# A two-layer hybrid decoder trunk: x, weights and parameters laid out by the host before the launch

## The chip, the cores and the metric

The kernel runs on one core of a Trainium2 chip. The metric is the time of one execution on the device, in microseconds (us). Engines are named as in the profile: PE multiplies matrices (PEld loads its stationary operand beside it), DVE and ACT work on vectors, POOL is a third vector engine, SP issues most of the loads.

## The reference

The input x is 512 tokens by 1024 features in float32. Each of two layers does the following.

- RMSNorm, then one input projection whose columns feed four groups of heads: forgetting attention (fox), gated linear attention (gla), multi-head latent attention with a rotary key (mla), and a Mamba-2 SSD mixer with a causal convolution (ssm).
- The four results, 256 wide each, go side by side through one output projection and are added to x.
- RMSNorm, a SwiGLU FFN with 2816 hidden units, and a second addition to x.

A final RMSNorm ends it. What the change touches is how the first of these steps begins:

```python
def rmsnorm(x, g):
    y = x * lax.rsqrt(jnp.mean(x * x, axis=-1, keepdims=True) + EPS)
    return y * g
x1 = rmsnorm(x, norm1[l]) @ w_in[l]      # 512 x 1024 times 1024 x 3000
```

## The kernel before, in words

**Tiling.** The residual x is held turned, as eight tiles `xT[k]` of 128 features by 512 tokens. Every projection is made of matmuls with a 128x128 block of the weight as the stationary operand and 512 tokens moving, summed over k in one bank of PSUM. To keep float32 accuracy, each operand is split into a high part and the remainder (`h`, `l`), and each block takes three matmuls: high by high, low by high, high by low (`prod`, L369 to L371).

**Weights.** `Weights` (L250) is a queue of units of up to 128x1024 numbers, in order of use. A unit is loaded by SP into one of two raw tiles `wr`. It is then split: ACT copies the high part `wh` (L276), DVE subtracts to get `wl` (L277), into one of three pairs of tiles. `get` keeps two units split ahead. A unit that is one 128-column block of `w_in` is read from the array as it lies, in pieces of 128 numbers (512 bytes). Small columns (gates, low rank, rotary key) are gathered by six loads into a unit that POOL has set to zero (`add_small`, L312). The two up-projections of mla are split in pieces, which also puts their columns in order (`add_mla`, L281 and L282).

**The start.** The order of the first steps on PE, DVE and ACT is written out by hand in the string `FIRST`. `T` turns one 128-feature chunk of x with four PE transposes against the identity, since x lies token by token (L917). `N` makes the two parts of a chunk, times the gain of the norm (L417, L418). `A` and `B` split the first and second half of one of the two first units. `P` does the three matmuls of one chunk for one of the two first projections. `X` and `Y` copy the turned chunk to `xT`; `Q` squares a chunk on ACT and adds it up on POOL (L941, L943); `R` makes the token-wise factor r of the norm from the sum. The factor is applied behind the projections, so PE can begin before it is known; it is spread over the partitions by one PE matmul (`spread`, L444). Before all this PE does seven warm-up matmuls on ones (`WARM`, L142).

**Parameters.** The gains and other vectors come as rows, are turned on PE and copied (`prn` at L143, `load_vectors` from L178: ten loads issued by ACT). The biases and the SSD's A and D come as four broadcasts to 128 partitions, issued by POOL (L199). Positions are loaded by POOL too (L227).

**Order.** Behind the written-out block, a planner puts instructions into each engine's order, by its own estimate of when each can run; projections run on PE while generators (`Runner`) feed the mixers' steps in between. SP's loads run in the order in which they are issued.

Of the kernel before, what the change touches and what calls it, by code (L numbers as in the profile page):

```python
# [20 lines left out]
P = 128  # L22
T = 512
# [16 lines left out]
WARM = 7  # L40
# [5 lines left out]
FIRST = """T0 T1 N0 A0 T2 N1 P00 B0 T3 N2 P01 Y0 P02 N3 T4 P03 A1 Y1 T5 P10 B1 N4 P11 P12 X2 P13 N5 Q0 T6 P04 P14 Q1 Q2  # L46
X3 N6 P05 P15 T7 Q3 Q4 W2 X4 N7 P06 P16 Q5 X5 Q6 P07 P17 Q7 X6 X7 W3 R0"""
# [11 lines left out]
def _consts():  # L59

    c = np.zeros((P, 2), np.float32)
    d = np.arange(P) % 32
    c[:, 0] = _rope_inv()[d % 16]
    c[:, 1] = np.where(d < 16, -1.0, 1.0)
    return c
# [14 lines left out]
def trunk(tc, I, out, depth=2):  # L80
# [7 lines left out]
    with ExitStack() as es:  # L88
# [26 lines left out]
        xb = []  # L115

        def load_x(n):
            for k in range(len(xb), n):
                t = tmp("a", f"x_{k}")
                nc.sync.dma_start(t.rearrange("p (b c) -> p b c", b=NB),  # L120
                                  I["x"][0].rearrange("(b p) c -> p b c", p=P)[:, :, blk(k)])
                xb.append(t)

        load_x(2)

        prn = tmp("f", "prn", P, parts=16)
        nc.scalar.dma_start(prn, I["norm1"].rearrange("l (k p) -> (l k) p", p=P))
        pcn = cp.tile([P, 16], F32, name="pcn")
        pcv = cp.tile([P, 98], F32, name="pcv")
        col = lambda i: pcn[:, i:i + 1] if i < 16 else pcv[:, i - 16:i - 15]  # L130
# [12 lines left out]
        PE.transpose(pps[:, 0:16], prn, ident[0:16, 0:16])  # L143
        V.tensor_copy(pcn, pps[:, 0:16])
# [33 lines left out]
        def load_vectors():  # L178
            prow = tmp("f", "prow", P)
            for r0, src in ((0, I["norm2"].rearrange("l (k p) -> (l k) p", p=P)),  # L180
                            (16, I["ssm_conv_w"].rearrange("l t (k p) -> (l t k) p", p=P)),
                            (64, I["ssm_conv_b"].rearrange("l (k p) -> (l k) p", p=P)),
                            (76, I["gla_gate_b"]),
                            (78, I["mla_q_norm"].rearrange("l (k p) -> (l k) p", p=P)),
                            (82, I["mla_kv_norm"]),
                            (84, I["ssm_norm"].rearrange("l (k p) -> (l k) p", p=P)),
                            (88, I["final_norm"].rearrange("(k p) -> k p", p=P))):
                n = src.shape[0]
                nc.scalar.dma_start(prow[r0:r0 + n, :], src)
            for half in range(2):  # L190
                nc.scalar.dma_start(prow[96:98, blk(half, 64)], I["gla_out_norm"])
            ps = ps_mix("ppv")
            PE.transpose(ps[:, 0:98], prow[0:98], ident[0:98, 0:98])
            V.tensor_copy(pcv, ps[:, 0:98])


        bc = cp.tile([P, 2, 16], F32, name="bc")
        for i, nm in enumerate(("fox_f_bias", "ssm_dt_bias", "ssm_A_log", "ssm_D")):
            nc.gpsimd.dma_start(bc[:, :, 4 * i:4 * i + 4], I[nm].unsqueeze(0).broadcast_to((P, 2, 4)))  # L199
        rc = cp.tile([P, 2], F32, name="rc")  # L200


        dcol = cp.tile([P, 2, 2], F32, name="dcol")
# [5 lines left out]
        def gate_constants():  # L209
            V.memset(gsgn[:, 0:4], -1.0)  # L210
            V.memset(gsgn[:, 4:8], 1.0)
            V.tensor_tensor(gbias, bc[:, :, 0:8], gsgn.unsqueeze(1).broadcast_to((P, 2, 8)), op=ALU.mult)
            V.memset(gfac, -1.0)
            S.activation(gfac[:, :, 4:8], bc[:, :, 8:12], AF.Exp)
            V.tensor_scalar(gfac[:, :, 4:8], gfac[:, :, 4:8], -1.0, None, op0=ALU.mult)
            for c in range(2):
                for hh in range(2):
                    V.tensor_copy(dcol[blk(hh, 64), :, c:c + 1],
                                  bc[blk(hh, 64), :, 12 + 2 * c + hh:13 + 2 * c + hh])
# [30 lines left out]
        class Weights:  # L250


            def __init__(self):
                self.queue, self.loaded, self.ready, self.n = [], [], [], 0

            def add(self, load, nk, ncol, pack=None):
                self.queue.append((load, nk, ncol, pack))

            def load(self):
                load, nk, ncol, pack = self.queue.pop(0)  # L260
                i, n = self.n, nk * ncol
                self.n += 1
                raw = wp.tile([P, 1024], F32, tag="wr", bufs=RAWS, name=f"wr{i}")
                load(raw[:, :n].rearrange("p (k c) -> p k c", k=nk), raw)
                self.loaded.append((raw, i, nk, ncol, pack))

            def split(self, pieces=1):

                if not self.loaded:
                    self.load()  # L270
                raw, i, nk, ncol, pack = self.loaded.pop(0)
                n = nk * ncol
                h, lo = (wp.tile([P, 1024], F32R, tag=f"w{c}", bufs=PARTS, name=f"w{c}{i}") for c in "hl")
                if pack is None:
                    for c in (blk(j, n // pieces) for j in range(pieces)):
                        S.copy(h[:, c], raw[:, c])  # L276
                        V.tensor_tensor(lo[:, c], raw[:, c], h.bitcast(F32)[:, c], op=ALU.subtract)  # L277
                        yield h, lo
                else:
                    for dst, src in pack:  # L280
                        S.copy(dst(h), src(raw))  # L281
                        V.tensor_tensor(dst(lo), src(raw), dst(h.bitcast(F32)), op=ALU.subtract)  # L282
                    nk, ncol = pack_shape[nk, ncol]
                    n = nk * ncol
                self.ready.append(tuple(t[:, :n].rearrange("p (k c) -> p k c", k=nk) for t in (h, lo)))

            def prefetch(self, n):
                while (self.queue or self.loaded) and len(self.ready) < n:
                    for _ in self.split():
                        pass  # L290
# [6 lines left out]

        pack_shape = {(2, 384): (2, 512), (1, 512): (1, 512)}

        def add_block(*srcs):  # L300

            nk = sum(s.shape[0] for s in srcs) // P

            def load(v, raw):
                k = 0
                for s in srcs:
                    n = s.shape[0] // P
                    nc.sync.dma_start(v[:, k:k + n, :], s.rearrange("(k p) c -> p k c", p=P))
                    k += n
            W.add(load, nk, srcs[0].shape[1])  # L310

        def add_small(l):  # L312
            def load(v, raw):
                G.memset(raw, 0.0)
                w = I["w_in"][l].rearrange("(k p) c -> p k c", p=P)
                for dst, src, n in ((0, FF, 4), (4, SDT, 4), (32, GG, 16), (64, MKR, 32), (96, MKR + 16, 16),
                                    (112, MKR, 16)):
                    nc.sync.dma_start(v[:, :, dst:dst + n], w[:, :, src:src + n])
            W.add(load, KC, P)

        def add_mla(l):

            v8 = lambda t, n: t[:, :8 * n].rearrange("p (k c) -> p k c", k=8)
            cut = lambda a, n, w: (lambda t: v8(t, w)[:, :, a:a + n])
            W.add(lambda v, raw: nc.sync.dma_start(v, I["mla_w_uq"][l].rearrange("(k p) c -> p k c", p=P)), 2, 384,
                  [(cut(d0, n, 128), cut(s0, n, 96)) for d0, s0, n in ((0, 0, 96), (96, 80, 16), (112, 64, 16))])

            dst = lambda i: (lambda t: t[:, blk(i, 256)].rearrange("p (h c) -> p h c", h=4))
            src = lambda i: (lambda t: t[:, :512].rearrange("p (h c) -> p h c", h=4)[:, :, blk(i, 64)])
            W.add(lambda v, raw: nc.sync.dma_start(raw[:, :512], I["mla_w_ukv"][l]), 1, 512,  # L330
                  [(dst(i), src(i)) for i in range(2)])

        def layer_weights(l):
            win, wout = I["w_in"][l], I["w_out"][l]
            cols = lambda c0: add_block(win[:, c0:c0 + P])
            for c0 in FRONT_COLS[:2]:
                cols(c0)
            add_small(l)
            for c0 in FRONT_COLS[2:] + (FK, FQ):
                cols(c0)  # L340
            tok = lambda c0: (add_block(win[0:512, c0:c0 + 256]), add_block(win[512:1024, c0:c0 + 256]))
            tok(FV)
            for c0 in (FK + P, FQ + P, MCKV, MCQ, MCQ + P, GQ, GK):
                cols(c0)
            tok(GV)
            add_mla(l)
            for i in range(4):
# [856 lines left out]
```

## Time and profile before

| | us |
|---|---|
| median of 3 runs | 1283.63 (1283.08 to 1284.28) |
| the profiled execution, its own time | 1284.61 |
| its span, from the first to the last instruction | 1282.9 |
| PE busy | 1253.4 (98%) |
| DVE busy | 697.2 (54%) |
| ACT busy | 534.5 (42%) |
| POOL busy | 195.5 (15%) |

The busy times of engines overlap. The mean granted clock of PE is 0.989 of full speed. 109.41 MB are moved in 207396 packets, 203896 of them smaller than 2 KB, at a mean of 85 GB/s.

### The profile page before, as it was taken

The page shows a single profiled execution, that of the slowest core. Times are in us where ns is not written, and L with a number is a line of the kernel's source. Part 1 is how long each engine was busy: PE and PEld are TensorE (multiplying, and loading weights), DVE is VectorE, ACT ScalarE, POOL GpSimd, SP SyncE. Part 2 cuts the span into 40 slices and gives each one's busy share as a digit, 9 for nine tenths or more (in the row PEclk, how much of TensorE's full clock was granted, in tenths as well). Part 3 has the DMA queues.
Part 4 walks back from the last instruction along what each step waited for, and adds up shares of the span by engine and source line. Part 5 has one row for each costly group of instructions (what it writes and reads, how often), then busy time and mean ns, then how long its engine had stood idle before and what let it go on. Part 6 is the DMA issues. An engine that isn't in the chain of part 4 may idle for free.

```text
span 1282.9 us, 16334 instructions
## 1 busy us (share of the span) xinstructions
PE 1253.4 (98%) x6414; PEld 1017.2 (79%) x6414; DVE 697.2 (54%) x1144; ACT 534.5 (42%) x890; POOL 195.5 (15%) x178
## 2 busy tenths in 40 slices
PE   7999999999999999999999999999999999999997
PEld 5788787678888888888888877777688888888886
DVE  5786698584343344343457677966644334433444
ACT  4456774743221222223444577565432222212232
POOL 4112221031110110011201022000311001101111
PEclk7999999999999999999999999999899999999999
DMA  7333212122333333333343221112233333333331
GB/s 135 102 99 83 58 34 79 38 75 86 99 99 99 97 90 92 100 99 91 90 98 95 69 81 53 60 42 66 66 99 99 99 99 99 89 100 99 95 90 70
DMA packets 207396, 109.41 MB, mean 85 GB/s; under 512 B 16872, under 2 KB 203896, under 8 KB 207320
## 3 DMA queue, kind: packets, MB, share of 16 engines
q1 hardware_dynamic: 206304, 107.95, 29.6%
q0 software_dynamic: 816, 0.36, 0.4%
q8 instruction: 50, 0.82, 0.3%
q14 instruction: 26, 0.21, 0.1%
q10 hardware_dynamic: 200, 0.06, 0.0%
HBM read 106.19 MB, written 2.10 MB: 84 GB/s over the span
## 4 chain that ended last, share of the span: by engine, by line
PE 90%; DVE 5%; ACT 2%; DMA 1%; issue 1%; POOL 1%; SPq 0%; DVEq 0%; ACTq 0%; POOLq 0%
PE u L369 6%; PE u L370 6%; PE u L371 6%; PE g L371 6%; PE g L369 6%; PE g L370 6%; PE d L369 5%; PE d L370 5%; PE d L371 5%; PE ft L370 3%; PE ft L369 3%; PE ft L371 3%; PE sm L745 1%; PE oa L370 1%; PE oa L369 1%; PE oa L371 1%
## 5 line engine op out<-in xcount | busy, mean ns | idle before, releaser
L276 ACT CAST wh<-wr 128x1024 fp32r<-128x1024 f32 (+2 forms) x202 | 206.8, 1025 | 567.4 <-issue 256.2
L277 DVE TENSOR_TENSOR wl<-wr,wh 128x1024 fp32r<-128x1024 f32 (+2 forms) x202 | 245.9, 1218 | 78.9 <-ACT wh L276 78.6
L369 PE MATMUL d<-uh,wh 128*128 128x512 f32 x296 | 115.1, 389 | 0.0
L370 PE MATMUL d<-uh,wl 128*128 128x512 f32 x296 | 115.1, 389 | 0.0
L371 PE MATMUL d<-ul,wh 128*128 128x512 f32 x296 | 115.1, 389 | 0.0
L1163 DVE TENSOR_TENSOR ft<-u,fs 128x512 f32<-128x512 f32 x44 | 30.4, 692 | 133.1 <-PE u L371 127.4
L1177 DVE TENSOR_TENSOR xT<-xT,d 128x512 f32<-128x512 f32 x40 | 27.5, 687 | 104.6 <-PE d L371 104.6
L1160 POOL TENSOR_TENSOR fs<-fs,n_0r 128x512 f32<-128x512 f32 x22 | 38.3, 1743 | 279.4 <-ACT fs L1159 279.4
L1160 POOL TENSOR_TENSOR fs<-fs,n_1r 128x512 f32<-128x512 f32 x22 | 38.1, 1734 | 280.5 <-ACT fs L1159 280.5
L371 PE MATMUL g<-n_1l,wh 128*128 128x512 f32 x176 | 69.0, 392 | 2.3 <-DVE n_1l L418 2.3
L371 PE MATMUL g<-n_0l,wh 128*128 128x512 f32 x176 | 68.7, 390 | 2.3 <-DVE n_0l L418 2.3
L369 PE MATMUL g<-n_0h,wh 128*128 128x512 f32 x176 | 69.0, 392 | 0.8 <-ACT n_0h L417 0.8
L369 PE MATMUL g<-n_1h,wh 128*128 128x512 f32 x176 | 69.0, 392 | 0.8 <-ACT n_1h L417 0.8
L370 PE MATMUL u<-n_1h,wl 128*128 128x512 f32 x176 | 69.4, 395 | 0.0
L369 PE MATMUL u<-n_1h,wh 128*128 128x512 f32 x176 | 69.4, 394 | 0.0
L371 PE MATMUL u<-n_1l,wh 128*128 128x512 f32 x176 | 69.3, 394 | 0.0
L370 PE MATMUL u<-n_0h,wl 128*128 128x512 f32 x176 | 69.2, 393 | 0.0
L369 PE MATMUL u<-n_0h,wh 128*128 128x512 f32 x176 | 69.1, 393 | 0.0
L371 PE MATMUL u<-n_0l,wh 128*128 128x512 f32 x176 | 69.0, 392 | 0.0
L370 PE MATMUL g<-n_1h,wl 128*128 128x512 f32 x176 | 68.5, 389 | 0.0
L370 PE MATMUL g<-n_0h,wl 128*128 128x512 f32 x176 | 68.5, 389 | 0.0
L371 PEld LDWEIGHTS d<-ul,wh 128*128 128x128 f32 x296 | 55.6, 188 | 11.6
(640 smaller groups left out, 2862.2 us busy)
## 6 DMA issues: line engine op xcount, KB each, us to landing
wr<-in_w_in_dram SPq DMA_DIRECT2D x46, 512.0 KB
wr<-in_w_gate_dram SPq DMA_DIRECT2D x44, 512.0 KB
wr<-in_w_up_dram SPq DMA_DIRECT2D x44, 512.0 KB
wr<-in_w_down_dram SPq DMA_DIRECT2D x32, 448.0 KB
wr<-in_w_down_dram SPq DMA_DIRECT2D x16, 512.0 KB
wr<-in_w_out_dram SPq DMA_DIRECT2D x16, 256.0 KB
wr<-in_w_out_dram SPq DMA_DIRECT2D x8, 512.0 KB
x<-in_x_dram SPq DMA_DIRECT2D x8, 256.0 KB
```

What stands on the lines that cost most here:

```text
L276: S.copy(h[:, c], raw[:, c])
L277: V.tensor_tensor(lo[:, c], raw[:, c], h.bitcast(F32)[:, c], op=ALU.subtract)
L369: PE.matmul(ps, lhsT=wh[:, k, c0:c0 + P], rhs=ah, start=k == 0, stop=False)
L370: PE.matmul(ps, lhsT=wl[:, k, c0:c0 + P], rhs=ah, start=False, stop=False)
L371: last = PE.matmul(ps, lhsT=wh[:, k, c0:c0 + P], rhs=al, start=False, stop=k == n - 1)
L745: PE.matmul(ps[:, :n], lhsT=q[:d, blk(qb)], rhs=k[:d, :n], start=i == 0, stop=i == len(terms[h]) - 1)
L1160: G.tensor_tensor(s, s, r, op=ALU.mult)
L1163: V.tensor_tensor(t, pu, s, op=ALU.mult)
L1177: V.tensor_tensor(xT[m], xT[m], ps, op=ALU.add)
```

## The change

The host lays out the inputs before the launch. x comes as eight blocks of 128 features by 512 tokens. Weights come as one array of units in order of use, 128 rows of 1024 numbers (4 KB) each, with the small columns and the mla columns already in place. All parameters come as one array of 152 columns. In the kernel, the turning of x, of the parameters, the broadcasts and the gathering loads are gone. SP issues x chunks and halves of the first two units by turns. Warm-up matmuls are 14 and not 7. The written-out order changes; the squares are summed on DVE, behind the split of the third unit, and the sum over features is a PE matmul (`columns`) as in the second layer. Positions are loaded by ACT.

```diff
-WARM = 7
+WARM = 14
-FIRST = """T0 T1 N0 A0 T2 N1 P00 B0 T3 N2 P01 Y0 P02 N3 T4 P03 A1 Y1 T5 P10 B1 N4 P11 P12 X2 P13 N5 Q0 T6 P04 P14 Q1 Q2
-X3 N6 P05 P15 T7 Q3 Q4 W2 X4 N7 P06 P16 Q5 X5 Q6 P07 P17 Q7 X6 X7 W3 R0"""
+FIRST = """N0 A0 P00 N1 A1 P10 P01 P11 N2 P02 P12 B0 N3 P03 P13 B1 N4 P04 P14 N5 P05 P15 N6 P06 P16 N7 P07 P17 W2 Q0 Q1 Q2 Q3
+Q4 Q5 Q6 Q7"""
+def _unit(w):
+    k = w.shape[0] // P
+    return w.reshape(k, P, -1).transpose(1, 0, 2).reshape(P, -1)
+def _weights(I, depth=2):
+    units, shapes = [], []
+    def add(*ws):
+        u = np.concatenate([_unit(w) for w in ws], 1)
+        shapes.append((u.shape[1] // ws[0].shape[1], ws[0].shape[1]))
+        units.append(np.pad(u, ((0, 0), (0, 1024 - u.shape[1]))))
...
+    return np.stack(units), shapes
+        def load_x(k):
+            nc.sync.dma_start(xT[k], I["x"][k])
+        pcv = cp.tile([P, 176], F32, name="pcv")
+        nc.scalar.dma_start(pcv[:, :152], I["columns"])
...
-            nc.gpsimd.dma_start(posi, I["positions"].broadcast_to((P, T)))
-            nc.gpsimd.dma_start(rc, I["rope_const"])
+            nc.scalar.dma_start(posi, I["positions"].broadcast_to((P, T)))
...
+            def load(self, parts=1):
+                i, (nk, ncol) = self.n, shapes[self.n]
+                self.n += 1
                 raw = wp.tile([P, 1024], F32, tag="wr", bufs=RAWS, name=f"wr{i}")
+                self.loaded.append((raw, i, nk, ncol))
+                for c in (blk(j, nk * ncol // parts) for j in range(parts)):
+                    nc.sync.dma_start(raw[:, c], I["weights"][i][:, c])
+                    yield
...
-            def square(self, k):
+            def square(self, k, adds=None):
...
-                    (V if k == KC - 1 else G).tensor_tensor(self.acc, self.acc, sq, op=ALU.add)
+                    (adds or (V if k == KC - 1 else G)).tensor_tensor(self.acc, self.acc, sq, op=ALU.add)
+                    return square
...
-        W.load()
-        load_x(4)
-        W.load()
-        load_x(KC)
+        loads = [W.load(2), W.load(2)]
+        for k in range(KC):
+            load_x(k)
+            if k < 4:
+                next(loads[k % 2])
+        for w in loads:
+            list(w)
...
             elif op[0] == "Q":
-                sq = tmp("f", f"xq{k}") if k else acc
-                S.activation(sq, xb[k], AF.Square)
-                if k:
-                    return G.tensor_tensor(acc, acc, sq, op=ALU.add)
+                squares = norm.square(k, V)
+                return squares
 
         with tc.manual_schedule(engines=ORDERED):
-            squares = None
             for op in FIRST.split():
-                squares = first(op) or squares
-            r = norm.spread()
+                squares = first(op)
+        norm.columns()
+        r = norm.spread()
         selectors()
-        load_vectors()
         gate_constants()
```

## Rows read from the trace of the kernel before

**Rows 1.** The page, part 1: busy us, share of the span, instructions.
```profile
PE 1253.4 (98%) x6414; PEld 1017.2 (79%) x6414; DVE 697.2 (54%) x1144; ACT 534.5 (42%) x890; POOL 195.5 (15%) x178
```

**Rows 2.** Table by stretches: stretch, its length, busy by engine, PEclk, DMA share, GB/s.
```profile
5.80:11.50 5.70, 0.00 (x0) 0.00 (x0) 1.00 (x3) 1.04 (x3) 0.82 (x2) 0.71 1.08 158
...
16.40:21.80 5.40, 5.38 (x17) 4.50 (x18) 2.29 (x6) 2.98 (x6) 0.00 (x0) 0.50 0.84 173
...
21.80:38.00 16.20, 16.12 (x76) 12.81 (x75) 14.01 (x19) 9.45 (x15) 12.55 (x10) 1.00 0.59 122
38.00:39.60 1.60, 0.00 (x0) 0.00 (x0) 1.18 (x4) 0.23 (x2) 0.00 (x0) 1.00 0.70 96
39.60:85.00 45.40, 45.37 (x204) 36.90 (x205) 36.95 (x74) 22.14 (x28) 3.69 (x7) 1.00 0.40 106
...
280.00:290.00 10.00, 6.80 (x24) 4.71 (x23) 8.87 (x9) 3.15 (x5) 4.41 (x3) 0.90 0.36 105
644.80:655.70 10.90, 10.90 (x51) 9.03 (x49) 3.17 (x4) 2.66 (x4) 0.18 (x1) 1.00 0.50 108
```

**Rows 3.** The chain of waits in order of time: start us, us, what.
```profile
3.08 13.29 DMA x<-in_x_dram
...
85.24 0.87 PE xt L542 x8
...
655.83 0.79 PE n_1ms L435 x8
...
660.87 0.86 PE n_1sp L444 x2
...
708.18 0.87 PE xt L542 x8
```

**Rows 4.** Instructions in order of time, SP's issues and PE: start us, us, engine, line.
```profile
0.82 0.98 SPq L120 DMA_DIRECT2D x<-in_x_dram  x2
...
1.13 3.36 PE L142 MATMUL pps<-ones 128*128 128x128 f32 x14 [1.13 <-DVE ones L134]
...
4.64 1.14 PE L917 MATMUL xt<-ident,x 128*128 128x128 f32 x8
...
5.53 3.36 SPq L308 DMA_DIRECT2D wr<-in_w_in_dram  x1
...
8.94 8.25 SPq L120 DMA_DIRECT2D x<-in_x_dram  x4
...
16.42 1.11 PE L917 MATMUL xt<-ident,x 128*128 128x128 f32 x4 [2.48 <-DMA x<-in_x_dram]
```

**Rows 5.** DMA queues in 0:20, 2:4, 8:12 and 1276:1279: packets, MB, share of 16 engines.
```profile
DMA packets 7122, 3.13 MB, mean 157 GB/s; under 512 B 1065, under 2 KB 7122, under 8 KB 7122
...
q1 hardware_dynamic: 1010, 0.50, 84.5%
...
q0 software_dynamic: 77, 0.01, 58.1%
q1 hardware_dynamic: 1096, 0.55, 53.4%
...
q1 hardware_dynamic: 228, 0.43, 39.0%
```

**Rows 6.** Groups of instructions by line and shape, 0 to 42 us: busy us, mean ns.
```profile
L418 DVE SCALAR_TENSOR_TENSOR n_0l<-xt,pcn,n_0h 128x512 fp32r<-128x512 f32 x8 | 6.0, 749 | 5.9 <-ACT n_0h L417 5.8
L417 ACT ACTIVATE n_0h<-xt,pcn 128x512 fp32r<-128x512 f32 x8 | 5.5, 688 | 10.3 <-PE xt L917 10.3
...
L941 ACT ACTIVATE xq<-x 128x512 f32<-128x512 f32 x7 | 4.0, 622 | 0.0
...
L277 DVE TENSOR_TENSOR wl<-wr,wh 128x512 fp32r<-128x512 f32 x4 | 2.7, 686 | 4.5 <-ACT wh L276 4.5
L276 ACT CAST wh<-wr 128x512 fp32r<-128x512 f32 x4 | 2.5, 614 | 4.7 <-DMA wr<-in_w_in_dram 4.7
```

**Rows 7.** One line, L282, both layers: duration ns min/median/max, first and last start, forms.
```profile
L282 DVE TENSOR_TENSOR wl<-wr,wh x10: 267/415/1372, 173.5 to 813.2; 128x128 fp32r<-128x128 f32 x4, 128x256 fp32r<-128x256 f32 x4, 128x768 fp32r<-128x768 f32 x2
```

More of the change, by code (lines that the diff above doesn't have):

```diff
@@ L56, in _rope_inv @@
     return np.float32(10000.0) ** (-(np.arange(16, dtype=np.float32) / np.float32(16.0)))
[L59 to L65, printed above, removed]
+def _unit(w):
[7 more added lines that the diff above has]
+        units.append(np.pad(u, ((0, 0), (0, 1024 - u.shape[1]))))
+    for l in range(depth):
+        win, wout = I["w_in"][l], I["w_out"][l]
+        cols = lambda c0: add(win[:, c0:c0 + P])
+        for c0 in FRONT_COLS[:2]:
+            cols(c0)
+        small = np.zeros((D, P), np.float32)
+        for dst, src, n in ((0, FF, 4), (4, SDT, 4), (32, GG, 16), (64, MKR, 32), (96, MKR + 16, 16), (112, MKR, 16)):
+            small[:, dst:dst + n] = win[:, src:src + n]
+        add(small)
+        for c0 in FRONT_COLS[2:] + (FK, FQ):
+            cols(c0)
+        tok = lambda c0: (add(win[0:512, c0:c0 + 256]), add(win[512:1024, c0:c0 + 256]))
+        tok(FV)
+        for c0 in (FK + P, FQ + P, MCKV, MCQ, MCQ + P, GQ, GK):
+            cols(c0)
+        tok(GV)
+        uq = I["mla_w_uq"][l].reshape(256, 4, 96)
+        add(np.concatenate([uq, uq[:, :, 80:96], uq[:, :, 64:80]], 2).reshape(256, 512))
+        add(I["mla_w_ukv"][l].reshape(P, 4, 2, 64).transpose(0, 2, 1, 3).reshape(P, 512))
+        for i in range(4):
+            add(wout[768:1024, 256 * i:256 * i + 256], wout[0:256, 256 * i:256 * i + 256])
+        for r0 in (256, 512):
+            for i in range(2):
+                add(wout[r0:r0 + 256, 512 * i:512 * i + 512])
+        for j0, j1 in HID_PARTS:
+            for j in range(j0, j1):
+                add(I["w_gate"][l][:, j * P:j * P + P])
+                add(I["w_up"][l][:, j * P:j * P + P])
+            for m in range(KC):
+                add(I["w_down"][l, j0 * P:j1 * P, m * P:m * P + P])
+    return np.stack(units), shapes
@@ L77, in _pieces, with trunk @@
     return out
-def trunk(tc, I, out, depth=2):
+def trunk(tc, I, out, shapes, depth=2):
     nc = tc.nc
@@ L253, in __init__ @@
             def __init__(self):
[L254 to L261, printed above, removed]
+                self.loaded, self.ready, self.n = [], [], 0
+            def load(self, parts=1):
+                i, (nk, ncol) = self.n, shapes[self.n]
@@ L269, in split @@
                 if not self.loaded:
-                    self.load()
-                raw, i, nk, ncol, pack = self.loaded.pop(0)
+                    list(self.load())
+                raw, i, nk, ncol = self.loaded.pop(0)
                 n = nk * ncol
                 h, lo = (wp.tile([P, 1024], F32R, tag=f"w{c}", bufs=PARTS, name=f"w{c}{i}") for c in "hl")
[L274 to L284, printed above, removed]
+                for c in (blk(j, n // pieces) for j in range(pieces)):
+                    S.copy(h[:, c], raw[:, c])
+                    V.tensor_tensor(lo[:, c], raw[:, c], h.bitcast(F32)[:, c], op=ALU.subtract)
+                    yield h, lo
@@ L285, in split @@
                 self.ready.append(tuple(t[:, :n].rearrange("p (k c) -> p k c", k=nk) for t in (h, lo)))
             def prefetch(self, n):
-                while (self.queue or self.loaded) and len(self.ready) < n:
+                while (self.n < len(shapes) or self.loaded) and len(self.ready) < n:
                     for _ in self.split():
@@ L296, in trunk @@
         W = Weights()
[L298 to L331, printed above, removed]
@@ L359, in trunk @@
-        for l in range(depth):
-            layer_weights(l)
         def prod(ps, w, act, c0=0, ks=None, t=slice(0, T), nk=None):
@@ L1190 @@
     from concourse.bass_utils import run_bass_kernel_spmd
+    inputs = {n: np.asarray(inputs[n]) for n in _INS}
     nc = bacc.Bacc("TRN2", target_bir_lowering=False, num_devices=1, dynamic_dma_scratch_size=4096)
-    arrays = {f"in_{n}_dram": np.ascontiguousarray(inputs[n]) for n in _INS}
-    arrays["in_rope_const_dram"] = _consts()
-    I = {}
-    for n in _INS + ["rope_const"]:
-        a = arrays[f"in_{n}_dram"]
+    units, shapes = _weights(inputs)
+    laid = {"x": np.ascontiguousarray(inputs["x"][0].T).reshape(KC, P, T), "positions": inputs["positions"],
+            "columns": _columns(inputs), "gla_gate_w2": inputs["gla_gate_w2"], "weights": units}
+    arrays, I = {}, {}
+    for n, a in laid.items():
+        arrays[f"in_{n}_dram"] = a = np.ascontiguousarray(a)
         I[n] = nc.dram_tensor(f"in_{n}_dram", a.shape, mybir.dt.from_np(a.dtype), kind="ExternalInput").ap()
@@ L1200 @@
     with tile.TileContext(nc) as tc:
-        trunk(tc, I, out)
+        trunk(tc, I, out, shapes)
     r = run_bass_kernel_spmd(nc, [arrays], core_ids=[0])
```

104 lines of the change are left out of this document (18 added, 86 removed).

## The prediction

> **What bounds the kernel now.** I read the busy table first: PE is busy 98% of the 1282.9 us span [rows 1], so only time in which PE stands or runs at its lower clock can be won. Then the table by stretches, to find that time [rows 2]. Nearly all that this change can reach lies ahead of 40 us. PE does nothing from 5.8 to 11.5 us, runs at the lower of its two levels (granted 0.50, 1.2 GHz) from 16.4 to 21.8, goes at 1.00 (2.4 GHz) from 21.8, and stands once more from 38.0 to 39.6. Third, the chain of waits says why [rows 3]: its first long piece is 13.29 us of waiting for a load of x, issued at 3.08. Later, at 38.0, the sum of squares that POOL adds up is late.
>
> From about 40 us on PE is the bound. Layer 1 is the template for a front without waits. There the two first projections (48 matmuls) run from 644.8 without a gap to 655.83, that is 11.0 us, where the row sums of the norm begin; the transposes of the SSD part (xt of L542) begin at 708.18, 52.35 us later [rows 2, 3]. In layer 0 the same transposes begin at 85.24. From there both layers keep the same distance, so what the front gains is kept to the end. If the two projections end at time E and nothing stands after them, xt begins at E + 52.35. The gain is 85.24 - 52.35 - E = 32.9 - E, less new waits.
>
> **Why the loads are slow.** What must arrive, x (8 x 0.262 MB) and two weight units (2 x 0.524 MB), is 3.15 MB. In the first 20 us 3.13 MB were moved, 157 GB/s [rows 5]. Yet from 2 to 4 us 0.50 MB took 84.5% of 2 us of all engines, 296 GB/s while they worked. From 8 to 12 us SP's queue took 53.4% for 0.55 MB, and POOL's queue 58.1% (2.3 us of all sixteen engines) for 0.01 MB: the four broadcasts of the small parameters (L199). SP's issues show the same: the first two cost 0.98 us together, the four x loads issued at 8.94 took 8.25 us, 2.06 each [rows 4].
>
> **Part by part.**
> *Loads.* The broadcasts go; the parameters come as one load on ACT's queue. x and weight halves come by turns, twelve loads of 0.262 MB in rows of 2 KB. The trace has such rows only in the output: 0.43 MB in 39.0% of 3 us, 367 GB/s [rows 5]; they are writes, so this is the good end. x_0 was there by 4.64, when the first transposes ran [rows 4]. The other eleven need 11 x 0.71 = 7.9 us at 367 GB/s, 9.7 at 296, and 18.4 at the old mean of 157. So x_7 is there at 12.5, 14.4 or 23.0 us. I take 12.5 to 14.4, because the mean of 157 contains the broadcasts and 1024 row pieces per weight unit where there are now 128 per half.
>
> *PE in the front.* 32 transposes go. Fourteen warm-up matmuls replace seven. Seven were 14 instructions in 3.36 us, 0.24 each. Right after them eight transposes took 1.14 us (0.14 each), at 16.42 four took 1.11 (0.28) [rows 4]: the clock had risen by 4.64 and was lost in the idle time after 5.8. Twenty-eight instructions from 1.13 end at 7.85 if all go at 0.24, and at 6.25 if those after 4.64 go at half that. The first projection step needs x_0 and half of w_0: from 4.64 two ACT operations (0.69 + 0.61) and DVE's remainder (0.69) [rows 6], so 6.6. PE therefore runs without a hole from 1.13 into the projections, at the upper level. It starts them between 6.6 and 7.85 and needs 11.0 for them: E = 17.6 to 18.9; I take 18.2. Feeding keeps up: a chunk of x costs PE 11.0 / 8 = 1.38 us, DVE 0.75, ACT 0.69, and the loads 0.71 to 0.89, or twice that while halves of the weights come between. All of ACT's work is 8 x 0.69 + 4 x 0.61 = 8.0, DVE's 8 x 0.75 + 4 x 0.69 = 8.8, both below PE's 11.0. Gain so far 32.9 - 18.2 = 14.7.
>
> *The norm factor r.* POOL's seven adds go to DVE (0.69 each), behind the split of w_2 and beside eight squares on ACT (0.62 each) [rows 6], in the written order. With x_7 at 14.4, ACT ends N7 at 15.1, w_2 (twice a half, 1.2) at 16.3, the squares at 21.3; DVE's last add ends at 22.0. Row sums on PE are new in layer 0. In layer 1 it is 5.0 us from them to the spread matmul (655.83 to 660.87), with 0.86 for that and a copy [rows 3]. That makes r about 28.5, and its first product, which frees a bank, 29.2. PE has two more projections to do before it needs the bank: 18.2 + 2 x 5.5 = 29.2. So the cover is just enough; where the planner puts row sums and spread in PE's queue decides. The split of w_3 is the other tight one: its buffer is free at about 17.5, it is needed at 23.7, and behind the adds it ends at 23.4. Bounds: 0, as in layer 1, to 4.5 (row sums queued right behind the projections, 22.0 - 18.2, and some wait at the spread). Before, that wait was 1.6 [rows 2]. I take 0.9.
>
> *What is hidden.* ACT's ten small loads and their transposes (they fell after 38 us, and from 39.6 PE has 45.37 of 45.40 us of work [rows 2]), eight copies of x, POOL's memset for the small unit, four copies of D's columns: all stood beside PE's work or inside the stretch already counted; nothing more is taken for them. The positions load moves from POOL's to ACT's queue behind DVE's fourth product; the SiLU queued behind it on ACT waits for that same product, and PE asks for the angles' product only in the up-projections, behind the whole front: 0 to 0.5 us of ACT (an issue as the first x load's), 0 for PE.
>
> *The up-projections of MLA.* DVE's five pieces per layer (one of 1.37, two of 0.27, two of about 0.4 us [rows 7], 2.7 in all) become one of 1024 and one of 512 columns, 1.38 + 0.69: 0.6 less, twice. In that stretch DVE sets the pace in part. Bounds 0 to 1.2; I take 0.3, since PE is seldom out of work there.
>
> *All other weights.* They come in rows of 4 KB. From 39.6 to 85 us PE stood for 0.03 us in all, so shorter loads gain nothing; a loss begins where a load takes longer than the two units (2 x 5.5 us of PE) that are loaded ahead, against 3.3 us for 0.524 MB at 157 GB/s. I take 0.
>
> *Later clock.* From 280 to 290 PE works 6.80 of 10 us and the clock falls (0.90) [rows 2]. An earlier start can move this fall by a few tenths either way: 0, with about 1.5 either way in the range.
>
> **Sum.** 14.7 - 0.9 + 0.3 = 14.1 us off the profiled execution's own 1284.61 us: 1270.5. The median of the runs, 1283.63, lies 1.0 lower; the forecast is 1269.5.
>
> **Rivals.**
> 1. *The loads stay the pace.* If something other than the broadcasts held them, x_7 comes at up to 23.0; then N7 (0.69 + 0.75) and the last three matmuls (0.7) make E 25.1, a gain of 7.8 - 0.9 + 0.3 = 7.2: 1276.4. In between, 1272 to 1276. For it: the mean of 157 was also that of SP's large loads. Against: 296 GB/s from 2 to 4 us, and 58.1% for the broadcasts after it.
> 2. *r is late.* A stall of 2 to 4.5 us in place of 0.9: 1270.6 to 1273.1. For it: the old 1.6 us wait, and a chain that ends within tenths of its cover. Against: layer 1 has the same chain and no wait.
> 3. *The clock is lost again* between warm-up and projections, if w_0 comes some us later than x_0 (before, PE stood till 11.5). Then the 48 matmuls begin at 1.2 GHz, 0.43 us each for 0.23: half of them cost 5 us, all of them 10. 1274.5 to 1279.5.
> 4. *Slower: a load costs SP its issue whatever its rows.* If the 2.06 us are the price of one load and not of its 512 pieces, twelve end at 0.82 + 24.8 = 25.6, x_7 lands about 1.5 later, and E is 29.3: a gain of 3. At 3.36, what one weight unit cost SP at 5.53 [rows 4], E is 45 and the kernel is 12 us slower (1295). It turns at about 2.4 us per load. Against: 0.49 each for the first two. The Trainium skill speaks for it: the page "DMA: Bandwidth & Descriptors", section "Anatomy of one DMA — SWDGE (gpsimd) path", gives each DMA a fixed part of about 2 us on that path, and its "Rules for kernel authors" want 1 MiB and more per DMA. By that, taken for loads that don't overlap, I would estimate 2.6 us for each of the twelve, 31 us in all, and no gain. The trace says otherwise so far: two loads issued 0.49 us apart had both arrived when the eight transposes ran from 4.64 to 5.78.
> 5. *The planner arranges later work otherwise*, since its inputs change; a few us either way. I have no row for it.
>
> **How the numbers follow.** Forecast 0.60 (1267 to 1272), rival 1 0.12, rival 2 0.11, rival 3 0.08, rival 4 0.04, rival 5 with an outcome outside these 0.05. Range 1266 to 1276: the forecast, rival 2, most of rival 1 and the cheap end of rival 3. 0.2% is 2.6 us, about what a measurement of this kernel can tell from no change. All but rival 4 and part of 5 lie beyond it: faster 0.92, same 0.03, slower 0.05.
>
> **What would show it.** In the profile after: POOL's queue nearly empty before 12 us; x_7's chunk no longer on the chain; the granted clock at 1.00 without a break from before 8 us; the second projection's last matmul at 17.6 to 18.9; xt of L542 in layer 0 at about 71, in layer 1 still 622.9 later. An x load as the first long piece of the chain speaks for rival 1 or 4, a stretch at 0.50 after 8 us for rival 3, a PE wait ahead of the row sums or the spread for rival 2. A distance between the layers other than 622.9 makes the argument from the front wrong.

## The result, and the profile after

| | before | after |
|---|---|---|
| median, us | 1283.95 (1283.08 to 1284.57) | 1269.45 (1269.22 to 1269.87) |
| span of the profiled execution, us | 1282.9 | 1268.1 |
| mean granted clock of PE | 0.989 | 0.994 |

The ratio is 0.9888, with an interval of 0.9871 to 0.9905: 14.5 us less. The forecast was 1269.5.

The busy table of after [rows 1], and the transfers of the whole execution:

```profile
PE 1248.9 (98%) x6402; PEld 1014.5 (80%) x6402; DVE 694.0 (55%) x1132; ACT 533.5 (42%) x882; POOL 179.1 (14%) x163
...
DMA packets 32907, 109.99 MB, mean 87 GB/s; under 512 B 4096, under 2 KB 4256, under 8 KB 32832
```

PE's busy time is 4.5 us less, the transposes of x and the matmuls at the lower clock among it. The time in which PE stands is 10.3 us less (29.5 before, 19.2 after). The bytes are nearly the same (109.41 MB before), in a sixth of the packets. The table by stretches of after shows where the time was won [rows 2]. Its columns are the stretch, its length, busy time of PE, PEld, DVE, ACT and POOL, the granted clock, the share of the DMA engines, GB/s:

```profile
4.00:8.00 4.00, 4.00 (x21) 3.67 (x19) 2.83 (x6) 2.68 (x5) 0.00 (x0) 1.00 0.89 289
8.00:12.00 4.00, 3.85 (x17) 2.85 (x16) 2.41 (x7) 2.83 (x5) 0.00 (x0) 1.00 0.95 360
12.00:16.00 4.00, 3.74 (x16) 2.56 (x15) 4.00 (x9) 3.47 (x6) 0.00 (x0) 1.00 0.80 223
16.00:20.00 4.00, 4.00 (x20) 3.30 (x19) 3.69 (x6) 4.00 (x9) 0.00 (x0) 1.00 0.49 141
```

Before, PE stood from 5.8 to 11.5 us and ran at 0.50 from 16.4 to 21.8. Now it works at 1.00, with holes of 0.15 and 0.26 us of busy time in the two middle stretches (1.3 us by the starts of the matmuls, as shown below), and the loads arrive at 289 to 360 GB/s where 158 to 173 stood in before's rows.

The chain of waits of after, in order of time (start us, us, what) [rows 3]:

```profile
3.62 6.75 DMA xT<-in_x_dram
10.39 0.73 ACT n_0h L363
...
11.72 0.76 DVE n_0l L364
12.53 0.50 PE ft L317
...
24.46 0.79 PE n_0ms L382 x8
...
28.13 0.86 PE n_0sp L391 x2
...
71.96 0.87 PE xt L489 x8
...
283.50 0.86 PE n_0ms L407 x2
...
643.41 0.79 PE n_1ms L382 x8
...
695.74 0.87 PE xt L489 x8
...
906.08 0.86 PE n_1ms L407 x2
```

The transposes of the SSD part in layer 0 (xt) begin 13.28 us earlier (85.24 to 71.96), those of layer 1 12.44 us earlier. The steps between are found by setting each such row against its twin of before. The lead is 12.40 at the row sums of layer 0's second norm (283.50, before 295.90) and 13.82 at layer 1's (906.08, before 919.90). The last write of DVE begins 13.94 us earlier, and the output stores behind it take 0.9 us less: 14.8 of span.

Instructions of after in order of time (start us, us, engine, line) [rows 4]: the issue of a load costs SP 0.3 to 0.6 us, the warm-up runs into the projections, and these end at 19.3. The line at 11.31 and the last one are two steps on DVE that the part on the prediction comes back to.

```profile
0.82 0.39 SPq L174 DMA_DIRECT2D xT<-in_x_dram  x1
...
1.14 6.13 PE L195 MATMUL pps<-ones 128*128 128x128 f32 x28 [1.14 <-DVE ones L187]
1.26 0.42 SPq L282 DMA_DIRECT2D wr<-in_weights_dram  x1
...
4.78 2.48 SPq L174 DMA_DIRECT2D xT<-in_x_dram  x4
...
7.02 0.48 PE L315 MATMUL ft<-n_0h,wh 128*128 128x512 f32 x1
...
11.31 0.39 DVE L224 CAST gmask<-tri 64x64 int32<-64x64 f32 x2
11.75 2.72 ACT L363 ACTIVATE n_0h<-xT,pcv 128x512 fp32r<-128x512 f32 x4
...
17.39 4.66 DVE L375 TENSOR_TENSOR n_0acc<-n_0acc,n_0q 128x512 f32<-128x512 f32 x6
19.08 0.39 PE L317 MATMUL ft<-n_0l,wh 128*128 128x512 f32 x1
19.31 0.39 PE L315 MATMUL sm<-n_0h,wh 128*128 128x512 f32 x1
...
23.10 0.69 DVE L375 TENSOR_TENSOR n_0acc<-n_0acc,n_0q 128x512 f32<-128x512 f32 x1
```

### The profile page after: what moved, and what is told of

Same layout as the page of the kernel before. It is cut to its first block, busy times and chain, and to the rows that moved or that the text cites. A ratio compares the mean times of both kernels' runs of the same rounds, so it can differ in the third digit from the quotient of the medians.

```text
span 1268.1 us, 16210 instructions
## 1 busy us (share of the span) xinstructions
PE 1248.9 (98%) x6402; PEld 1014.5 (80%) x6402; DVE 694.0 (55%) x1132; ACT 533.5 (42%) x882; POOL 179.1 (14%) x163
## 4 chain that ended last, share of the span: by engine, by line
PE 92%; DVE 5%; ACT 2%; DMA 1%; issue 0%; POOL 0%; SPq 0%; DVEq 0%
PE u L315 6%; PE u L316 6%; PE u L317 6%; PE g L317 6%; PE g L315 6%; PE g L316 6%; PE d L315 5%; PE d L316 5%; PE d L317 5%; PE ft L317 3%; PE ft L316 3%; PE ft L315 3%; PE sm L692 1%; PE oa L316 1%; PE oa L315 1%; PE oa L317 1%
## 5 line engine op out<-in xcount | busy, mean ns | idle before, releaser
L293 ACT CAST wh<-wr 128x1024 fp32r<-128x1024 f32 (+2 forms) x206 | 210.3, 1023 | 567.1 <-issue 342.5
L294 DVE TENSOR_TENSOR wl<-wr,wh 128x1024 fp32r<-128x1024 f32 (+2 forms) x206 | 249.9, 1213 | 73.2 <-ACT wh L293 73.0
L315 PE MATMUL d<-uh,wh 128*128 128x512 f32 x296 | 115.1, 389 | 0.0
L316 PE MATMUL d<-uh,wl 128*128 128x512 f32 x296 | 115.1, 389 | 0.0
L317 PE MATMUL d<-ul,wh 128*128 128x512 f32 x296 | 115.1, 389 | 0.0
```

The lines of the kernel that those rows point to most:

```text
L315: PE.matmul(ps, lhsT=wh[:, k, c0:c0 + P], rhs=ah, start=k == 0, stop=False)
L316: PE.matmul(ps, lhsT=wl[:, k, c0:c0 + P], rhs=ah, start=False, stop=False)
L317: last = PE.matmul(ps, lhsT=wh[:, k, c0:c0 + P], rhs=al, start=False, stop=k == n - 1)
```

## The experiments

Each was timed beside the kernel before, in four to eleven executions. "Front" below is the start of layer 0's xt, 71.96 us in after and 85.24 in before. Several runs split the change into its parts: the broadcasts (1, 4, 5, 9, 10), the rows (2), the warm-up (3), the sum of squares (6, 12), the turning of x (7). Two try to better it (8, 11).

**1. The broadcasts put back.** After, with POOL's four broadcasts into a tile that nobody reads; the pad tile is smaller by as much.

```diff
-PAD = 72
+PAD = 40
+        old = cp.tile([P, 2, 16], F32, name="old")
+        for i, nm in enumerate(("fox_f_bias", "ssm_dt_bias", "ssm_A_log", "ssm_D")):
+            nc.gpsimd.dma_start(old[:, :, 4 * i:4 * i + 4], I[nm].unsqueeze(0).broadcast_to((P, 2, 4)))
```

> The changed kernel, with POOL's four broadcasts of the small parameters issued again into a tile that nothing reads (a padding tile is made smaller by as much). Theory A: these broadcasts held the engines that carry x, so they are what made the loads slow. Then the x chunks land later, the two first projections end at 22 to 25 us in place of 19.3, and the time is 3 to 6 us above the changed kernel's. Theory B: what was slow were the rows of 512 bytes (many pieces per load); with rows of 2 KB the broadcasts cost under 0.5 us.

Measured: 1281.71 us (1280.13 to 1282.5), ratio 0.998 (0.9971 to 0.9989): 12.3 of the 14.5 us are lost again. Two rows of its table by stretches, same columns:

```profile
8.00:12.00 4.00, 0.00 (x0) 0.00 (x0) 0.09 (x1) 0.72 (x1) 0.00 (x0) 0.91 0.98 176
12.00:16.00 4.00, 2.87 (x6) 2.04 (x7) 3.10 (x5) 3.03 (x5) 0.00 (x0) 0.50 0.82 309
```

From 8 to 12 us the DMA engines are 98% busy and move 176 GB/s (after: 360 at 95%). PE, which has done three matmuls by then, has nothing to do; it goes on at 13.13, at 0.50. Its queues from 4 to 8 us (packets, MB, share of 16 engines):

```profile
q1 hardware_dynamic: 320, 0.58, 42.8%
q0 software_dynamic: 47, 0.01, 36.9%
```

But the front is only 6.6 us late (78.58), near Theory A's 3 to 6; the other 5.7 us arise behind it. Run 9 separates the two.

**2. Rows of 512 bytes.** After, with x and the first two units loaded in 128-number pieces.

```diff
-            nc.sync.dma_start(xT[k], I["x"][k])
+            nc.sync.dma_start(xT[k].rearrange("p (b c) -> p b c", b=NB), I["x"][k].rearrange("b p c -> p b c"))
...
+                        nc.sync.dma_start(raw[:, c].rearrange("p (k c) -> p k c", k=KC // parts),
+                                          I["w_in"][0].rearrange("(k p) c -> p k c", p=P)[:, ks, GR + i * P:GR + i * P + P])
```

> The changed kernel, with x laid out so that each chunk is loaded in pieces of 512 bytes, and the two first units read from the weight array as it lies, in pieces of 512 bytes too; order, halves and all later units as in the changed kernel. Theory A: the length of the pieces hardly matters, 296 against some 310 GB/s: 0 to 1 us slower. Theory B: a load costs SP by its pieces, about 2 us for each of the twelve; the last chunk comes at about 25 us and the kernel is 5 to 9 us slower than the changed one.

Measured: 1270.14 us (1269.79 to 1271.16), ratio 0.9891 (0.9878 to 0.9905), front 72.49. The longer rows, the change's most visible part, are worth 0.5 us by the front and 0.7 by the medians. That is at the edge of what the runs tell apart: their ranges touch, and the two projections end no later than in after (at 19.1).

**3. Seven warm-up matmuls.** `WARM = 14` becomes `WARM = 7`.

> The changed kernel with 7 warm-up matmuls in place of 14. PE is out of work from 4.5 to 7.0 us, the first projection step still starts at 7.0. Theory A: the seven more hold or raise the clock, so without them the projections start at 1.2 GHz and the kernel is 2 to 6 us slower. Theory B: with the loads this fast the clock rises at once from the projections' own work or is not lost: under 1 us.

Measured: 1270.95 us (1270.62 to 1271.27), ratio 0.9896 (0.9883 to 0.991), front 73.27. A row of its table by stretches, and two matmuls in order of time:

```profile
8.00:12.00 4.00, 4.00 (x10) 2.93 (x10) 3.79 (x11) 3.89 (x7) 0.00 (x0) 1.00 0.99 370
```

```profile
10.16 0.63 PE L317 MATMUL ft<-n_0l,wh 128*128 128x512 f32 x1
10.59 0.63 PE L315 MATMUL ft<-n_0h,wh 128*128 128x512 f32 x1
```

In the same 4 us PE starts 10 matmuls where after has 17. They come every 0.43 us, the pace of 1.2 GHz, although the column of the granted clock says 1.00; in after they come every 0.23 us from 8.68 on. So here the column doesn't show the lower level, and the distance of the matmuls does. The loss is 1.3 us of front and 1.5 of the median, between what the two theories said.

**4. Before, without the broadcasts.** The same 32 columns come as one load of 128 rows of 128 bytes, from an array with every row written out, issued by ACT.

```diff
-        for i, nm in enumerate(("fox_f_bias", "ssm_dt_bias", "ssm_A_log", "ssm_D")):
-            nc.gpsimd.dma_start(bc[:, :, 4 * i:4 * i + 4], I[nm].unsqueeze(0).broadcast_to((P, 2, 4)))
+        nc.scalar.dma_start(bc.rearrange("p l c -> p (l c)"), I["bc"])
```

> The kernel before, with one alteration: the four broadcasts issued by POOL are one load of 128 rows of 128 bytes issued by ACT. Theory A: the broadcasts made the loads slow; the 13.3 us wait for x shrinks, the two first projections end 4 to 8 us sooner than 31.9, and the time falls by 3 to 7 us. Theory B: the pieces of 512 bytes made them slow; under 0.5 us.

Measured: 1277.53 us (1275.84 to 1278.48), ratio 0.9946 (0.9934 to 0.9959): 6.5 us less than before, with everything else left. Its table by stretches and its chain:

```profile
8.00:12.00 4.00, 2.93 (x13) 2.52 (x14) 2.61 (x4) 3.03 (x6) 0.95 (x1) 0.72 1.18 289
```

```profile
2.40 6.63 DMA x<-in_x_dram
...
26.54 2.16 POOL ssq L942
...
78.10 0.87 PE xt L541 x8
```

The load of x on the chain takes 6.63 us where it took 13.29 [rows 3], with the old layout and its short pieces. What is late next is POOL's sum of squares.

**5. The broadcasts issued by ACT.** As run 1, with `nc.scalar.dma_start` in place of `nc.gpsimd.dma_start`.

> The changed kernel with the same four broadcasts as in the first experiment, into a tile that nothing reads, but issued by ACT and not by POOL. Theory A: it is POOL's queue (its descriptors are made in software) that held the engines, so from ACT's queue the broadcasts cost under 1 us. Theory B: it is the shape, 128 rows of two pieces of 16 bytes from one address, so that the queue does not matter: 10 to 13 us slower than the changed kernel, as from POOL.

Measured: 1282.4 us (1278.8 to 1283.32), ratio 0.9986 (0.9977 to 0.9995), front 78.55: what run 1 gave. So it isn't POOL's queue. Its queues from 4 to 8 us (packets, MB, share of 16 engines):

```profile
q1 hardware_dynamic: 304, 0.54, 51.6%
...
q10 hardware_dynamic: 773, 0.01, 10.0%
```

ACT's queue (q10) shows 10% for the broadcasts, where POOL's showed 36.9% in run 1, and the harm is the same. All queues together show only 62% here. The share of a queue is thus not the price of its transfers; the fall of SP's queue is (0.54 MB here, 0.58 in run 1, 1.15 in after, in the same 4 us). The Trainium skill, page "DMA: Bandwidth & Descriptors", section "Issuing engines are not separate DMA queues", says that all queues share the same sixteen engines. Runs 1 and 5 agree: moving the broadcasts to another queue changed 0.7 us, within their spread.

**6. The squares added on POOL.** `norm.square(k, V)` becomes `norm.square(k, G)`.

> The changed kernel with the seven adds of the squares on POOL and not on DVE. Theory A: POOL's adds of 1.3 to 2.3 us end at 28 us or later (22.1 on DVE), the row sums come after the cover of two projections has run out, and PE stands: 2 to 6 us slower. Theory B: the factor r is early enough either way: under 0.5 us.

Measured: 1275.74 us (1274.73 to 1276.23), ratio 0.9937 (0.9925 to 0.9949), front 78.26. The row sums in order of time, the spread on the chain, then the table by stretches:

```profile
25.73 1.87 PE L382 MATMUL n_0ms<-ones,n_0acc 128*128 128x1 f32 x8 [4.41 <-POOL n_0acc L375]
```

```profile
33.23 0.86 PE n_0sp L391 x2
```

```profile
20.00:24.00 4.00, 1.31 (x6) 0.75 (x4) 0.00 (x0) 1.16 (x2) 3.77 (x4) 1.00 0.00 0
24.00:28.00 4.00, 2.27 (x9) 2.21 (x10) 0.37 (x2) 0.17 (x1) 2.11 (x3) 0.51 0.00 0
```

POOL's last add ends at 25.7, only 1.9 us behind DVE's in after (23.79). PE stands for 4.41 us at the row sums, which wait for that add, although 13 of the 24 matmuls of the projection `sm` are still to do: they stand behind the row sums in its queue, where in after only two do. Then its matmuls come 0.43 us apart till 30.6, and the spread comes at 33.23, against 28.13 in after. So 6.3 us of the gain go again, as Theory A's range has it. But the cover of two projections had not run out, as Theory A says; the row sums stood too early in PE's queue.

**7. x turned on PE.** After, with the old layout of x, 32 transposes and the copies in the written order.

```diff
+            if op[0] == "T":
+                xps.append((ps_acc if k % 2 else ps_proj)(f"xt_{k}"))
+                for b in range(NB):
+                    PE.transpose(xps[k][:, blk(b)], xb[k][:, blk(b)], ident)
...
-                norm.chunk(k)
+                norm.chunk(k, xps[k])
```

> The changed kernel with x as the reference has it, loaded in pieces of 512 bytes and turned by 32 PE transposes, with the copies to xT on ACT and DVE; weights, parameters, order of loads, warm-up and the sum on DVE as changed. Theory A: with the loads fast PE and DVE are the pace of the front, so the turning costs 3 to 6 us. Theory B: PE waits for loads anyway and the turning falls into holes: under 1 us.

Measured: 1274.82 us (1274.12 to 1275.94), ratio 0.993 (0.9918 to 0.9943), front 76.45: 5.4 us by the medians, 4.5 by the front. It contains the transposes, the copies, and the shorter pieces of x.

**8. Second halves later.** After, with the second halves of the first units loaded behind x_3 and split later, and a line that was to place the selectors behind the squares.

```diff
-FIRST = """N0 A0 P00 N1 A1 P10 P01 P11 N2 P02 P12 B0 N3 P03 P13 B1 N4 ...
+FIRST = """N0 A0 P00 N1 A1 P10 P01 P11 N2 P02 P12 N3 P03 P13 B0 B1 N4 ...
-            if k < 4:
-                next(loads[k % 2])
+            if k < 2:
+                next(loads[k])
+            if k == 3:
+                for w in loads:
+                    list(w)
...
+        with tc.issue_after(squares.ins):
+            selectors()
```

> The changed kernel with the second halves of the two first units loaded and split behind chunk 3 of x and not between chunks 1 and 4, and the masks for the selectors made behind the squares. Theory A: the 1.8 us for which PE stands between 8 and 14.2 us are waits for chunks 1 to 5 (their loads share the engines with halves that nobody needs yet, their split stands behind those halves and the masks on DVE): 0.7 to 1.5 us faster than the changed kernel. Theory B: the loads as a whole set the pace and their order does not matter: within 0.3 us.

Measured: 1268.97 us (1267.91 to 1269.96), ratio 0.9882 (0.9866 to 0.9897), front 72.03. No difference that this resolves. Two lines in order of time, of ACT and of DVE:

```profile
7.87 0.62 ACT L293 CAST wh<-wr 128x512 fp32r<-128x512 f32 x1 [1.67 <-DMA wr<-in_weights_dram]
...
14.25 0.28 DVE L226 TENSOR_TENSOR sel<-ident 40x128 fp32r<-40x128 f32 x1
```

The selectors did not move: DVE still makes their masks between 10.70 and 14.53 (11.11 to 15.01 in after), ahead of the squares. So only the later halves were tried. PE's wait went to another place: its fourth matmul starts at 8.54 and its fifth at 9.27, for the first half of the second unit, whose split ACT begins at 7.87.

**9. The control: own addresses.** As run 1, same tile, pad, queue and piece size (1024 pieces of 16 bytes), but each row is read from its own place in an array with every row written out.

```diff
-            nc.gpsimd.dma_start(old[:, :, 4 * i:4 * i + 4], I[nm].unsqueeze(0).broadcast_to((P, 2, 4)))
+            nc.gpsimd.dma_start(old[:, :, 4 * i:4 * i + 4], I["spread"][i])
```

> The changed kernel with four loads from POOL of the same shape as the broadcasts (128 rows of two pieces of 16 bytes, into a tile that nothing reads), but each row read from its own address: the host lays the parameters out 128 times. Theory B1: it is the one address that holds the engines, 256 reads of the same 32 bytes in each of four loads; with own addresses the time is within 1 us of the changed kernel. Theory B2: it is the number of small pieces; 10 to 13 us slower than the changed kernel, as with the broadcasts.

Measured: 1275.18 us (1273.24 to 1275.32), ratio 0.9932 (0.992 to 0.9945). Its queues from 4 to 8 us, its table by stretches and its chain:

```profile
q1 hardware_dynamic: 584, 1.07, 85.5%
q0 software_dynamic: 90, 0.01, 7.9%
```

```profile
8.00:12.00 4.00, 2.98 (x12) 2.25 (x13) 2.90 (x5) 3.51 (x6) 0.13 (x1) 1.00 1.01 365
```

```profile
72.27 0.87 PE xt L492 x8
...
698.93 0.87 PE xt L492 x8
```

The front is 0.3 us later than in after, against 6.6 in run 1. So neither the count nor the size of the pieces nor POOL's queue is to blame, but that all 128 partitions read the same addresses; why that is slow, no run shows. Against this control the broadcasts of run 1 cost 1281.71 - 1275.18 = 6.5 us, as much as run 4 gained by taking them away. PE's lower clock behind the wait is in that price.

Yet the control is 5.7 us slower than after, which by its time fits neither theory, with a front just as good, as B1 has it; layer 1's xt comes 626.66 us after layer 0's, in after 623.78. The groups of instructions by line, whole span (busy us, mean ns), first after and then the control:

```profile
L315 PE MATMUL d<-uh,wh 128*128 128x512 f32 x296 | 115.1, 389 | 0.0
```

```profile
L318 PE MATMUL d<-uh,wh 128*128 128x512 f32 x296 | 117.0, 395 | 0.0
```

Every matmul of the FFN's down projection takes (117.0 - 115.1) / 296 = 6.4 ns more. Three such groups of 296 make 5.7 us, as much as the medians differ (the two profiled executions differ by 5.1). The gate projection's median goes only from 389 to 390 ns. Runs 1, 5 and 10 have this tile and pad too and show 395; all others, before included, 389. What they share is where tiles lie: by the order in which the pools are opened, those between the extra tile and the pad lie 128 bytes further. The weights are among these and `uh`, `ul` are not, while both operands of the gate projection are. That the changed distance between the operands is the reason is argued and was not tried. What the runs show is that the 5.7 us go with the extra tile and pad, whatever is loaded into them.

**10. One broadcast in one piece.** As run 9, but one load by POOL of one row of 128 bytes to 128 partitions: 128 reads of one address.

```diff
+        old = cp.tile([P, 32], F32, name="old")
+        nc.gpsimd.dma_start(old, I["row"].broadcast_to((P, 32)))
```

> The changed kernel with one broadcast load from POOL into a tile that nothing reads: all 32 parameters lie side by side, so that it reads one address 128 times, in pieces of 128 bytes, where the four loads read 1024 times. Both theories, one address and number of pieces, expect about an eighth of the cost: 1 to 2 us slower than the changed kernel. Under 0.5 us would say that it is not a price per read.

Measured: 1279.39 us (1275.72 to 1279.86), ratio 0.9963 (0.9951 to 0.9976), front 75.42. Its row from 8 to 12 us:

```profile
8.00:12.00 4.00, 1.44 (x4) 0.94 (x5) 2.33 (x4) 2.95 (x5) 0.00 (x0) 0.90 1.03 375
```

SP's queue from 4 to 8 us:

```profile
q1 hardware_dynamic: 500, 0.92, 75.5%
```

The front loses 3.1 us against the control (1 to 2 were expected), with an eighth of the reads of run 1, which loses 6.3. So even one small broadcast hurts. But the front doesn't measure how much was held up. From 4 to 12 us SP's queue moves 2.52 MB in the control, 2.41 here and 1.27 in run 1: 0.11 MB less here, 1.25 less there. The loss here begins with one late chunk: ACT takes x_1 at 8.89 (6.11 in the control), PE stands till 10.24, and its matmuls then come 0.43 us apart till 14.5. One of the five executions took 1275.72 us, hardly more than the control, and two points don't give a law.

**11. The order of PE changed too.** Run 8, and in `FIRST` the first unit's second product `P01` before `A1 P10 P11`.

> The changed kernel with the late second halves and late masks of an earlier experiment, and PE's order turned so that the second step of the first projection comes before the first step of the second. Theory A: the 0.5 us for which PE waits at 8.3 us for the second unit's first half goes too: 0.6 to 1.3 us faster than the changed kernel. Theory B: the wait moves to the next step: as the kernel with late halves alone, some 0.5 us faster than the changed one.

Measured: 1268.44 us (1267.45 to 1269.81), ratio 0.9883 (0.9868 to 0.9898). From 8 to 12 us, and on the chain:

```profile
8.00:12.00 4.00, 4.00 (x19) 3.34 (x18) 3.87 (x9) 3.89 (x7) 0.00 (x0) 1.00 1.00 364
```

```profile
70.94 0.87 PE xt L489 x8
```

PE has no hole left in that stretch, the two projections end at 18.16, and the front is 1.0 us earlier. As in run 8, the selectors' masks did not move. The median is 1.0 us below that of after, but the ranges overlap, so it isn't shown to beat it.

**12. Before without broadcasts, squares added on DVE.** Run 4, with `V` in place of `G` for the seven adds.

> The kernel before without the broadcasts (one load of 128 rows on ACT in their place), and with the adds of the squares on DVE in place of POOL. Theory A: without the broadcasts the sum on POOL is what is late, so this takes 1.5 to 4 us off the time without the broadcasts (1274 to 1276). Theory B: DVE is as full there as POOL is slow (it copies x too), and nothing is won.

Measured: 1277.35 us (1276.4 to 1277.77), ratio 0.9951 (0.9938 to 0.9963), front 77.05. Against run 4 the median is 0.2 us lower, while the ratio to before is higher (0.9946 there): nothing that the runs resolve. The front is 1.05 us earlier on the chain:

```profile
77.05 0.87 PE xt L541 x8
```

That lead is gone at the second norm of layer 1 (row sums at 912.80, in run 4 at 912.62). POOL's sum, which was on run 4's chain, is off it. From 12 to 40 us PE has no hole left, so its own work, x's transposes among it, sets the pace there.

## Why the prediction was right

**The front, 32.9 - E.** E was taken as 18.2 (17.6 to 18.9); the next product starts at 19.31, 1.1 us later than taken and 0.4 beyond the bound. PE entered the projections at 7.02, inside the forecast's 6.6 to 7.85, without a break and at 1.00. The 48 matmuls took 12.3 us and not 11.0: PE stood about 1.3 us, at 8.34 for `wl`, at 12.53 and 14.19 for `n_0l`. The step that failed is "Feeding keeps up". It set means against means (1.38 us of PE per chunk against 0.69 and 0.75), but a chunk's load, ACT's part and DVE's part come one behind the other. Where halves of the weights come between, its own figure for a load, twice 0.71 to 0.89, is above PE's 1.38. x_3's load (3.62 for 6.75 us) stands first on the chain; it landed at 10.37, where the forecast's rates give 8.9 to 10.0. And its 8.8 us of DVE leave out the selectors' masks, 1.4 us from 11.11 on, 0.6 of them between the end of x_3's `n_0h` (11.12) and the start of its `n_0l` (11.72). All this is the mild part of rival 1, and 1.1 us of its 6.9. Run 11 filled these holes by order alone, with the masks still there.

**The loads.** Forecast 296 to 367 GB/s and x_7 at 12.5 to 14.4. Measured 289 and 360; the last four chunks pass ACT without a wait from 11.75 to 14.47, so x_7 was there by about 13.8. That the mean of 157 "contains the broadcasts" was right, and runs 1, 4, 5 and 9 show it. That it also contains the pieces of 512 bytes was nearly without weight (run 2). The forecast read the harm off POOL's queue share of 58.1% [rows 5]; run 5 shows that this share is no measure.

**SP's issue (rival 4, slower).** The first load cost SP 0.39 us and the last four 2.48 together, not 2.06 each: the old price was not one of the load by itself. With the broadcasts put back (run 1) a single x load cost SP 3.18 us. The Trainium skill, page "DMA: Bandwidth & Descriptors", section "Rules for kernel authors", asks for 1 MiB and more per DMA; here twelve loads of 256 KB, issued one behind the other, came at 289 to 360 GB/s, so for loads that overlap the measurement decides against it.

**The factor r.** Forecast: last add ends at 22.0, r is ready at 28.5, its first product at 29.2, when the cover of two projections ends too; a stall of 0.9. Measured: six of the seven adds end at 22.05 (17.39 + 4.66), but the split of w_3 stands before the seventh, which ends at 23.79. From the row sums to the spread it is 3.7 us (24.46 to 28.13) and not the 5.0 of layer 1. So r is copied by 29.62 and its first product ends at 30.34, 1.1 us later than forecast; the cover, 11.0 us behind 19.31, is later by as much. From the end of the projections to xt it is 52.65 us for the template's 52.35: a stall of 0.3. Rival 2 fell, but two sizes that were off, a later add and a shorter chain, made up for each other, and that is luck. "Where the planner puts row sums and spread in PE's queue decides" was right: in after the last add ends 0.7 us ahead of the row sums' place on the chain, and in run 6, with it 1.9 us later and the row sums 11 matmuls earlier in the queue, PE stands at them for 4.4 us.

**The clock (rival 3).** It was never lost between warm-up and projections: the granted clock stays at 1.00 and the matmuls come every 0.23 us but for the holes. Run 3 shows what the longer warm-up pays for: 1.5 us.

**Behind the front.** The up-projections of MLA gave 0.3 us per layer where 0.3 was taken for both; the bound was 1.2. The later clock moved as the range allowed. Around the second norm of layer 0 the granted clock falls to 0.50 in both kernels, and 12 matmuls come 0.43 us apart in after, 7 in before; around that of layer 1 it is 6 and 11. So the lead falls from 13.5 to 12.4 at the first and rises from 12.8 to 13.8 at the second. With the 0.3 of MLA, that is why the distance between the layers is 623.78 and not 622.9. By the forecast's own sign, another distance makes the argument from the front wrong; these two terms account for the 0.84 us, so the argument holds up to what the clock moves, about 1 us either way. The output stores gave 0.9 us that had no term; before's stores moved at 367 GB/s [rows 5], and why they are shorter wasn't tried.

**The sum.** Forecast 14.7 - 0.9 + 0.3 = 14.1 on the profiled execution. Measured 13.3 for the front (r's 0.3 in it), 0.6 for MLA, about 0 for the clock, 0.9 at the end: 14.8 of span, 14.5 of medians. The front came 0.5 us short of 13.8, and 0.3 of MLA and 0.9 at the end more than made up for it. For the profiled execution 1270.5 was forecast and 1269.87 measured; the forecast of the median hit within 0.1 us because the median lies 0.4 below that execution and not 1.0. So the hit is partly luck.

**What the parts are worth** by the runs: broadcasts 6.5, sum of squares on DVE 6.3 in the new order, turning x 5.4, warm-up 1.5, rows 0.7. They add up to 20.4 and not 14.5. Taken away from after, each loss holds the whole of the wait that then ends last, and in runs 1, 3 and 6 the lower clock behind it; added to before, the sum on DVE gained nothing that the runs resolve (run 12).

## What to carry to other kernels

In a front, look first for small loads that read one address on every partition, and let the host write the rows out: the price isn't on their queue's line but in what all other loads move. Price a part by taking it out of the finished version and by adding it to the old one, since the two differ where the next wait is close behind. Where an engine waits with work left, look at the order of its queue, as at the row sums of run 6. An experiment that adds a tile needs a control with the same tile, for the placement alone can cost as much as the effect.

## What the hardware showed that was not expected

- Four broadcasts of 16 KB in all cost 6.5 us of the kernel from POOL's queue and 7.2 from ACT's, each against the control, PE's lower clock behind the wait included. The same pieces from own addresses cost the front 0.3 us; one broadcast of 128 bytes per partition costs it 3.1 against that control.
- Twelve loads in 512-byte pieces cost at the median only 0.7 us more than in 2 KB rows, at the edge of what the runs tell apart.
- Tiles placed 128 bytes further went with 6.4 ns more for each matmul of one group (395 for 389 ns), 5.7 us in all; the reason is open.
- The column of the granted clock can say 1.00 while matmuls come at the pace of 1.2 GHz (0.43 us each in run 3).
